# One trunk layer on one Trainium2 core: the first weight sums of the feed-forward computed during the output projection, low parts on VectorE, the first norm's vector spread by matmuls

## The chip, the core and the metric

The kernel runs on one core of a Trainium2 chip. Five engines work side by side, each with its own in-order instruction stream: TensorE (PE; its weight loads are listed apart as PEld), VectorE (DVE), ScalarE (ACT), GpSimd (POOL) and SyncE (SP), which here only issues DMA transfers. The metric is the device time of one execution in microseconds (us); lower is better.

## The reference, cut to what matters

```python
h = rmsnorm(x, norm_mix_pre)                      # x is 1024 x 1024, float32
proj = h @ w_in                                   # feeds convolution branch, attention, gates
...                                               # convolution branch, stick-breaking attention
merged = sigmoid(g_conv) * conv_out + sigmoid(g_att) * att_out
x = x + rmsnorm(merged @ w_out, norm_mix_post)    # output projection
h = rmsnorm(x, norm_ffn_pre)
gate, up = split(h @ w_ffn_up)                    # D_FF = 2816 = 22 blocks of 128
ff = (silu(gate) * up) @ w_ffn_down
x = x + rmsnorm(ff, norm_ffn_post)
```

## The kernel before

Every float32 product is made from three matmuls on rounded parts. An operand X is split into a high part (ScalarE copies X to the rounded type) and a low part (X minus the high part, a subtraction on VectorE or GpSimd); a step then adds high by high, high by low and low by high in PSUM. `mm3` writes these, twelve 128x512 matmuls for a product over four 128-row blocks.

The order of work is partly written out and partly made by a scheduler. Up to the feed-forward, the framework orders each engine's instructions from the program. From `up` on, the engines are wrapped in `Ordered`, so that the instructions keep the order in which the code issues them.

**First norm** (L148 to L190). `fetch(0)` loads the first 128 rows of x in two halves (`xts[0]`), the identity for transposes (`ident`) and the gain vector `gpre`, which one DMA copies to all 128 partitions; all are on SP's queue. `pre(tb)` squares block tb on ScalarE (L174, the sums go to `sst`), GpSimd takes the power to -0.5 (`pr`, L107), and VectorE multiplies by `pr` and `gpre` (L177). `transpose_split` transposes on PE and splits into `hH` and `hL`; `v_block` makes the first products `psv` (L139 to L141).

**Output projection** (L685 to L840). For each block tb of 128 tokens, `out_steps` makes `po`, and `post(tb)` adds the normed result to x (`x1`, L727 and L728) and writes the second normed block (`xr`, L736). `operands(tb - 2)` transposes an older block (`flip`). The feed-forward is a seven-product scheme on 2x2 blocks (Strassen's kind), so blocks 4 to 7 do not only give `hH`/`hL` but also the sums t1, t2 and t3: for each of these four blocks VectorE makes `s1`, `s2`, `s3` (L779 to L786), ScalarE rounds them (L788), and the low parts are taken at L789, t2's on VectorE, those of t1 (kept in `hL`) and t3 on GpSimd. `fetch_gate`, `prep_a` and `split` load and split the first gate weights `rg`; while `lows[0]` is GpSimd, all these low parts `wl` (L804, L835) are on GpSimd. PE meanwhile makes the first two of the seven products for f = 0, 1 and 2 (`early`).

**Feed-forward, up** (`up(f)`, 22 rounds). Round f has the products m5, m3, m6, m7, m4 besides its early m1 and m2 (for f > 0: m6, m5, m7, m3, m4). Their weights are sums of the gate and up blocks `rg` and `ru`: `sums_12` and `sums_34` (L894 to L900) followed by `split_12` and `split_34`. For f = 0 these stand under a high priority behind the output projection. `make_t4`, in round 0, makes the operand t4 from t2 and B21: twelve subtractions and additions `da`, `db` and four low parts on VectorE. Product m4 of round 0 needs it, and a free PSUM bank that VectorE's addition `u` gives back. From here on every engine's instruction has line L940.

**Last norm** (`evacuate`, last branch). For each of the last four blocks VectorE adds `c12` (tile `du`), ScalarE squares it (`junk`), VectorE multiplies it in place by the gain `gpo`, GpSimd takes the root, and VectorE scales and adds before the store.

Of the kernel before, what the change touches and what calls it, by code (L numbers as in the profile page):

```python
# [15 lines left out]
P = 128  # L16
# [21 lines left out]
def layer_kernel(ctx, tc, x, vecs, dww, gains, ident_d, mask_d, wv, wi, wbr, wo, wu, wdq, wd, out):  # L38
# [109 lines left out]
    vts = []  # L148
    with pool("prep") as pp:
        gpre = pp.tile([P, D], F32, name="gpre")  # L150
        wvt = []
        G.memset(mhalf, -0.5)
        xts = {}

        def parts_of(tb):
            return [slice(0, HALF), slice(HALF, D)] if tb == 0 else [slice(0, D)]

        def fetch(tb):
            xts[tb] = w4("xt")[:, 0:D]
            for cs in parts_of(tb):  # L160
                SP.dma_start(out=xts[tb][:, cs], in_=x[tb * P:(tb + 1) * P, cs])
            if tb == 0:
                SP.dma_start(out=ident, in_=ident_d)
                SP.dma_start(out=gpre, in_=gains[0:1, :].broadcast_to([P, D]))

        def pre(tb):
            if tb > 1:
                fetch(tb)
            xt = xts[tb]
            parts = parts_of(tb)  # L170
            junk = pp.tile([P, D], BF16, name="junk", tag="junk", bufs=1)
            sst = small("sst", 2)
            for n, cs in enumerate(parts):
                A.activation(out=junk[:, cs], in_=xt[:, cs], func=AF.Square, scale=ROOT, accum_out=sst[:, n:n + 1])  # L174
            r = power_of(sst[:, 0:1], 1, sst[:, 1:2] if tb == 0 else None)
            for cs in parts:
                V.scalar_tensor_tensor(out=xt[:, cs], in0=xt[:, cs], scalar=r, in1=gpre[:, cs], op0=ALU.mult, op1=ALU.mult)  # L177

        fetch(0)
        pre(0)  # L180
        fetch(1)
        transpose_split(psz, "z", xts[0], 0)
        wvt.append(load_w(wv[0, 0], pp, sub=V))
# [249 lines left out]
    def bank(nm):  # L433
        return ps8.tile([P, HALF], F32, name=nm, tag="d")
# [323 lines left out]
    def operands(tb):  # L758
        ps = slice((tb % 4) * P, (tb % 4) * P + P)

        def at_(t):
            return [o[:, :, ps] for o in t]

        def as_f32(t):
            return t.bitcast(F32)

        if tb < 4:
            for half, t in ((0, B11), (1, B21)):
                tp = flip(tb, half)
# [12 lines left out]
        tp = flip(tb, 1)
        A.activation(out=b22[0], in_=tp, func=AF.Copy)
        V.tensor_tensor(out=s2, in0=tp, in1=s1, op=ALU.subtract)
        V.tensor_tensor(out=b22[1], in0=tp, in1=as_f32(b22[0]), op=ALU.subtract)
        V.tensor_tensor(out=s3, in0=tp, in1=s3, op=ALU.subtract)  # L786
        for (h, l), src, eng in ((t2, s2, V), (t1, s1, G), (t3, s3, G)):
            A.activation(out=h, in_=src, func=AF.Copy)  # L788
            eng.tensor_tensor(out=l, in0=src, in1=as_f32(h), op=ALU.subtract)  # L789

# [2 lines left out]

    early = {}
    rgs, rus, ops = {}, {}, {}
    lows = [G]

    def split(src, pl, n=1024, low=None, tag="w", bufs=2):  # L800
        wh = pl.tile([P, n], F32R, name="wh", tag=f"{tag}h", bufs=bufs)
        wl = pl.tile([P, n], F32R, name="wl", tag=f"{tag}l", bufs=bufs)
        A.activation(out=wh, in_=src, func=AF.Copy)  # L803
        (low or lows[0]).tensor_tensor(out=wl, in0=src, in1=wh.bitcast(F32), op=ALU.subtract)  # L804
        return wh, wl

    def fetch_gate(f):
# [24 lines left out]
    raw2, wh2, wl2 = [op_.tile([P, 1024], dt, name=nm, tag="wh", bufs=6) for nm, dt in (("rg2", F32), ("wh2", F32R), ("wl2", F32R))]  # L832
    SP.dma_start(out=raw2, in_=wu[2])
    A.activation(out=wh2, in_=raw2, func=AF.Copy)
    G.tensor_tensor(out=wl2, in0=raw2, in1=wh2.bitcast(F32), op=ALU.subtract)  # L835
    ops[2] = {1: ((wh2, wl2), 0), 2: ((wh2, wl2), HALF)}
    operands(NT - 2)
    for f in range(3):
        early[f] = [bank("m1"), bank("m2")]
        prod(early[f][0], *ops[f][1], B11)  # L840
        if f == 2:
            pin[0] = True
            operands(NT - 1)
        prod(early[f][1], *ops[f][2], B21)
# [45 lines left out]
    def sums_12(f):  # L890
        rg, ru = rgs[f], rus[f]
        s12s[f] = fp.tile([P, 1024], F32, name="s12", tag="s", bufs=1)
        s1, s2 = s12s[f][:, 0:HALF], s12s[f][:, HALF:1024]
        V.tensor_tensor(out=s1, in0=ru[:, 0:HALF], in1=ru[:, HALF:1024], op=ALU.add)  # L894
        V.tensor_tensor(out=s2, in0=s1, in1=rg[:, 0:HALF], op=ALU.subtract)

    def sums_34(f):
        rg, ru, s2 = rgs[f], rus[f], s12s[f][:, HALF:1024]
        V.tensor_tensor(out=rg[:, 0:HALF], in0=rg[:, 0:HALF], in1=ru[:, 0:HALF], op=ALU.subtract)
        V.tensor_tensor(out=rg[:, HALF:1024], in0=rg[:, HALF:1024], in1=s2, op=ALU.subtract)  # L900

    def split_12(f):
        w = split(s12s[f], fp)
        ops[f][5], ops[f][6] = (w, 0), (w, HALF)

    def split_34(f):
        w = split(rgs[f], fp)
        ops[f][7], ops[f][3] = (w, 0), (w, HALF)

    def prep_c(f):  # L910
        ops[f][4] = (split(rus[f][:, HALF:1024], fp, HALF, tag="c", bufs=1), 0)

# [15 lines left out]
        for k, da in zip(ks, das):  # L928
            V.tensor_tensor(out=T4[1][:, k, :], in0=da, in1=T4[0][:, k, :].bitcast(F32), op=ALU.subtract)

    quads, s12s = {}, {}


    class Ordered:
# [222 lines left out]
    def root(sst):  # L1157
        return power_of(sst[:, 0:1], 1, sst[:, 1:2])
# [7 lines left out]
    def evacuate(i, p, ps):  # L1166
# [110 lines left out]
```

## Time and profile before

| | us |
|---|---|
| median of 3 runs | 1417.72 (1417.61 to 1420.14) |
| the profiled execution: its own time | 1417.84 |
| the profiled execution: span from first to last instruction | 1416.0 |
| PE busy in the span | 1363.2 (96%) |
| DVE busy | 1063.1 (75%) |
| ACT busy | 527.0 (37%) |
| POOL busy | 87.0 (6%) |

The profile is one execution. A busy share is a mean over stages. A row of the timeline gives an instruction's start, its duration, the engine, the line, what it writes and reads, and in brackets how long the engine had been idle and what ended that. "xt<-in_x" means that xt is written from in_x; buffer numbers are left out of names there.

### The profile page before, as it was taken

To read this page: it belongs to the slowest core of one execution; us is meant where nothing else is said; L and a number is where in the kernel's file an instruction comes from. 1 tells how busy PE (TensorE), PEld (TensorE's weight loads), DVE (VectorE), ACT (ScalarE), POOL (GpSimd) and SP (SyncE) were. 2 spreads that over 40 slices of the span, in tenths; PEclk is the share of its full clock that TensorE was granted. 3 is DMA by queue.
4 is the path that set the end of the run, shared out by engine and by line. 5 is a ranking of instruction groups with operands and counts; after the bars stand their busy time and mean duration, and the time that the engine had idled before them with its cause. 6 is when DMAs were issued, how large, how long until landed. Compare 5 with 4: busy or idle time off the path is not lost.

```text
span 1416.0 us, 17251 instructions
## 1 busy us (share of the span) xinstructions
PE 1363.2 (96%) x6412; PEld 1116.4 (79%) x6412; DVE 1063.1 (75%) x1560; ACT 527.0 (37%) x863; POOL 87.0 (6%) x208
## 2 busy tenths in 40 slices
PE   6999999999999999999998899999999999999997
PEld 6876787787877888888887678888888888788886
DVE  6599988886999967236549898888877876655565
ACT  6466656553102126123334323222222222533432
POOL 2100100000000000000117000000000000000102
PEclk9999999999999999999999999999999999999999
DMA  6011001100102121114322254444444434985373
GB/s 229 24 30 38 23 23 34 42 31 24 44 25 72 39 74 37 52 45 142 133 89 90 104 194 171 171 165 162 139 152 171 171 127 156 349 292 195 116 265 107
DMA packets 62403, 160.97 MB, mean 114 GB/s; under 512 B 6384, under 2 KB 17904, under 8 KB 62320
## 3 DMA queue, kind: packets, MB, share of 16 engines
q1 hardware_dynamic: 62032, 158.83, 32.9%
q8 instruction: 50, 0.82, 0.2%
q10 hardware_dynamic: 288, 1.05, 0.2%
q14 instruction: 33, 0.27, 0.1%
HBM read 117.65 MB, written 40.11 MB: 111 GB/s over the span
## 4 chain that ended last, share of the span: by engine, by line
PE 74%; DVE 16%; issue 3%; ACT 3%; DMA 2%; POOL 1%; SPq 0%; DVEq 0%; POOLq 0%; ACTq 0%
PE m L940 26%; PE md L940 13%; PE pg L82 4%; PE pg L80 4%; PE pg L79 4%; PE pb L82 2%; DVE R L262 2%; PE pb L80 2%; PE pb L79 2%; PE psg L82 2%; DVE R L257 2%; PE psg L80 2%; DVE p L469 2%; PE psg L79 2%; DVE aL L323 2%
## 5 line engine op out<-in xcount | busy, mean ns | idle before, releaser
L940 PE MATMUL m<-t,wh 128*128 128x512 f32 x528 | 133.8, 395 | 4.4 <-DVE u L940 2.9
L940 PE MATMUL m<-hH,wh 128*128 128x512 f32 x328 | 130.6, 398 | 4.4 <-ACT wh L803 4.4
L940 PE MATMUL m<-hL,wh 128*128 128x512 f32 x328 | 130.1, 397 | 0.0
L940 PEld LDWEIGHTS m<-t,wh 128*128 128x128 f32 x528 | 99.1, 188 | 29.2 <-issue 4.0
L940 PE MATMUL md<-wh 128*128 128x512 f32 x308 | 120.2, 390 | 1.1 <-ACT wh L940 1.1
L940 PE MATMUL md<-wl,wh 128*128 128x512 f32 x308 | 120.1, 390 | 0.9 <-DVE wl L940 0.9
L940 ACT ACTIVATE c<-c 128x512 f32<-128x512 f32 x44 | 27.8, 633 | 243.2 <-DVE c L940 243.2
L73 DVE TENSOR_TENSOR wl<-wraw,wh 128x1024 fp32r<-128x1024 f32 (+1 forms) x60 | 64.1, 1074 | 57.3 <-ACT wh L72 38.8
L72 ACT ACTIVATE wh<-wraw 128x1024 fp32r<-128x1024 f32 (+1 forms) x60 | 56.4, 945 | 123.7 <-PE pg L80 30.4
L79 PE MATMUL pg<-hH,wh 128*128 128x512 f32 x256 | 100.6, 393 | 0.0
L80 PE MATMUL pg<-hL,wh 128*128 128x512 f32 x256 | 99.7, 390 | 0.0
L940 PE MATMUL md<-wh,wl 128*128 128x512 f32 x308 | 97.4, 390 | 0.0
L940 DVE TENSOR_TENSOR wl<-ra,wh 128x1024 fp32r<-128x1024 f32 (+1 forms) x42 | 48.5, 1155 | 62.6 <-ACT wh L940 62.5
L940 PE MATMUL m<-hH,wl 128*128 128x512 f32 x328 | 89.8, 396 | 0.4 <-POOL wl L804 0.4
L469 DVE SCALAR_TENSOR_TENSOR p<-u,dw,p 128x513 f32<-128x513 f32 (+1 forms) x116 | 78.8, 737 | 0.0
L940 PEld LDWEIGHTS m<-hH,wh 128*128 128x128 f32 x328 | 62.2, 190 | 19.3 <-ACT wh L803 4.8
L940 PEld LDWEIGHTS m<-hH,wl 128*128 128x128 f32 x328 | 62.1, 189 | 15.2 <-POOL wl L804 0.8
L940 PEld LDWEIGHTS m<-hL,wh 128*128 128x128 f32 x328 | 62.2, 190 | 14.0
L940 ACT ACTIVATE wh<-ra 128x1024 fp32r<-128x1024 f32 (+1 forms) x42 | 41.4, 986 | 84.6 <-PE md L940 56.4
L940 PE MATMUL m<-t,wl 128*128 128x512 f32 x264 | 71.6, 394 | 0.0
L940 PEld LDWEIGHTS md<-wl,wh 128*128 128x128 f32 x308 | 57.8, 188 | 13.8 <-DVE wl L940 1.3
L940 PEld LDWEIGHTS md<-wh 128*128 128x128 f32 x308 | 57.8, 188 | 13.6 <-ACT wh L940 1.5
(233 smaller groups left out, 3231.7 us busy)
## 6 DMA issues: line engine op xcount, KB each, us to landing
ra<-act SPq DMA_DIRECT2D x35, 512.0 KB, 6.5
wraw<-in_wi SPq DMA_DIRECT2D x32, 512.0 KB, 3.6
rg<-in_wu SPq DMA_DIRECT2D x23, 512.0 KB, 4.8
ru<-in_wu SPq DMA_DIRECT2D x22, 512.0 KB, 5.6
q<-in_wdq SPq DMA_DIRECT2D x22, 512.0 KB, 6.4
wsum<-q SPq DMA_DIRECT2D x22, 512.0 KB, 2.6
act<-sa SPq DMA_DIRECT2D x44, 256.0 KB, 2.5
rb<-wsum SPq DMA_DIRECT2D x20, 512.0 KB, 9.7
```

What stands on the lines that cost most here:

```text
L72: A.activation(out=wh, in_=raw, func=AF.Copy)
L73: (sub or low_of[0]).tensor_tensor(out=wl, in0=raw, in1=wh.bitcast(F32), op=ALU.subtract)
L79: PE.matmul(ps, lhsT=lh, rhs=rh, start=(first and j == 0), stop=False)
L80: PE.matmul(ps, lhsT=lh, rhs=rl, start=False, stop=False)
L82: PE.matmul(ps, lhsT=ll, rhs=rh, start=False, stop=(last and j == n - 1))
L257: V.tensor_tensor_scan(out=R[:, 3:3 + n][:, ::-1], data0=d, data1=d, initial=1.0, op0=ALU.mult, op1=ALU.bypass)
L262: V.tensor_tensor_scan(out=R[:, 4:4 + n][:, ::-1], data0=d, data1=d, initial=carry, op0=ALU.mult, op1=ALU.bypass)
L323: V.tensor_tensor(out=flat[1][:, 0:n * P], in0=tpf, in1=flat[0][:, 0:n * P].bitcast(F32), op=ALU.subtract)
L469: V.scalar_tensor_tensor(out=to if last is None else last, in0=u[:, k:k + n], scalar=w, in1=to, op0=ALU.mult, op1=ALU.add)
L940: return lambda *a, **k: tc.keep_in_program_order(fn(*a, **k))
```

## The change

Four things change.

1. The gain vector of the first norm arrives as one row (`grow`, 4 KB on one partition). Two float32 matmuls of a row of ones with it spread it into two PSUM banks (`gps`); ScalarE copies these into `gpre`. Block 0 is multiplied by the PSUM banks themselves, the other blocks by `gpre`.
2. In `operands`, the low parts of t1 and t3 are taken by VectorE, in the order t1, t2, t3. `split` always uses VectorE for the low part, and so does the split of `rg2`. GpSimd is left with the powers to -0.5 and, in the last norm, with eight multiplications.
3. For f = 0 the up block is loaded into the output projection's pool (`ru0`), `sums_12(0)` and `sums_34(0)` are issued around `operands(6)`, and `split_12(0)` ahead of the early products of f = 1. `split_34(0)` stays where it was. The right half of the up block is loaded a second time behind it (`ru`), as `prep_c(0)` needs it unsummed.
4. In the last norm the multiplication by `gpo` writes another tile (`c22`) and no longer the tile that ScalarE squares.

```diff
-                SP.dma_start(out=gpre, in_=gains[0:1, :].broadcast_to([P, D]))
+                SP.dma_start(out=grow, in_=gains[0:1, :])
+                for n, cs in enumerate(parts_of(0)):
+                    PE.matmul(gps[n], lhsT=onerow, rhs=grow[:, cs], start=True, stop=True)
+                    A.activation(out=gpre[:, cs], in_=gps[n], func=AF.Copy)
...
-                V.scalar_tensor_tensor(out=xt[:, cs], in0=xt[:, cs], scalar=r, in1=gpre[:, cs], op0=ALU.mult, op1=ALU.mult)
+                V.scalar_tensor_tensor(out=xt[:, cs], in0=xt[:, cs], scalar=r, in1=gps[cs.start // HALF] if tb == 0 else gpre[:, cs], op0=ALU.mult, op1=ALU.mult)
...
-        for (h, l), src, eng in ((t2, s2, V), (t1, s1, G), (t3, s3, G)):
+        for (h, l), src in ((t1, s1), (t2, s2), (t3, s3)):
             A.activation(out=h, in_=src, func=AF.Copy)
-            eng.tensor_tensor(out=l, in0=src, in1=as_f32(h), op=ALU.subtract)
+            V.tensor_tensor(out=l, in0=src, in1=as_f32(h), op=ALU.subtract)
...
-        (low or lows[0]).tensor_tensor(out=wl, in0=src, in1=wh.bitcast(F32), op=ALU.subtract)
+        V.tensor_tensor(out=wl, in0=src, in1=wh.bitcast(F32), op=ALU.subtract)
...
-    G.tensor_tensor(out=wl2, in0=raw2, in1=wh2.bitcast(F32), op=ALU.subtract)
+    V.tensor_tensor(out=wl2, in0=raw2, in1=wh2.bitcast(F32), op=ALU.subtract)
     ops[2] = {1: ((wh2, wl2), 0), 2: ((wh2, wl2), HALF)}
+    rus[0] = op_.tile([P, 1024], F32, name="ru0", tag="wl", bufs=6)
+    SP.dma_start(out=rus[0], in_=wu[NFB])
+    sums_12(0, op_)
     operands(NT - 2)
+    sums_34(0)
     for f in range(3):
+        if f == 1:
+            split_12(0, wst)
...
-        fetch_up(0)
+        split_34(0)
+        rus[0] = fp.tile([P, 1024], F32, name="ru", tag="ru", bufs=2)
+        SP.dma_start(out=rus[0][:, HALF:1024], in_=wu[NFB, :, HALF:1024])
         fetch_up(1)
-        sums_12(0)
-        split_12(0)
-        sums_34(0)
-        split_34(0)
...
-            gained(1, c12[p], V)
-            finish(p, (c11[p], c12[p]), root(sst1[p]), xt)
+            V.tensor_tensor(out=c22[p], in0=c12[p], in1=gpo[:, HALF:D], op=ALU.mult)
+            finish(p, (c11[p], c22[p]), root(sst1[p]), xt)
```

VectorE's instructions at the start of the program, before. xt_103 and xt_118 are the first two blocks of x, `pv` the sum of squares that goes to GpSimd, `wl` the low part of a weight, `hL` that of a transposed half block:

```order
L105 TENSOR_SCALAR pv_112<-sst_109 128x1
L177 SCALAR_TENSOR_TENSOR xt_103<-xt_103,pr_114,gpre_101 128x512 x2
L103 TENSOR_SCALAR pv_143<-sst_141 128x1
L177 SCALAR_TENSOR_TENSOR xt_118<-xt_118,pr_145,gpre_101 128x1024
L73 TENSOR_TENSOR wl_137<-wraw_134,wh_136 128x1024
L118 TENSOR_TENSOR hL_79<-tp_120,hH_78 128x4x128
```

The same place after (the first two blocks are xt_108 and xt_127):

```order
L105 TENSOR_SCALAR pv_121<-sst_118 128x1
L103 TENSOR_SCALAR pv_152<-sst_150 128x1
L184 SCALAR_TENSOR_TENSOR xt_108<-xt_108,pr_123,gps_105 128x512
L73 TENSOR_TENSOR wl_146<-wraw_143,wh_145 128x1024
L184 SCALAR_TENSOR_TENSOR xt_108<-xt_108,pr_123,gps_106 128x512
L118 TENSOR_TENSOR hL_79<-tp_129,hH_78 128x4x128
L184 SCALAR_TENSOR_TENSOR xt_127<-xt_127,pr_154,gpre_101 128x1024
```

The multiplication of block 0 now stands behind the second block's sum of squares, and its second half behind the split of a weight. The whole first stage is woven anew in this way, on every engine; from the attention to the output projection the order of every engine is the same in both.

VectorE's instructions from the operands of the last block (`sums_6708`) to `make_t4`, before:

```order
L779 TENSOR_TENSOR sums_6708<-tp_6710,hH_78 128x512
L781 TENSOR_TENSOR sums_6708<-sums_6708,hL_79 128x512
L784 TENSOR_TENSOR sums_6708<-tp_6718,sums_6708 128x512
L785 TENSOR_TENSOR hL_79<-tp_6718,hH_78 128x4x128
L786 TENSOR_TENSOR sum3_6709<-tp_6718,sum3_6709 128x512
L789 TENSOR_TENSOR t2_5877<-sums_6708,t2_5877 128x4x128
L894 TENSOR_TENSOR s12_6812<-ru_6808 128x512
L895 TENSOR_TENSOR s12_6812<-s12_6812,rg_6152 128x512
L899 TENSOR_TENSOR rg_6152<-rg_6152,ru_6808 128x512
L900 TENSOR_TENSOR rg_6152<-rg_6152,s12_6812 128x512
L940 TENSOR_TENSOR c11_6833<-m2_6643,u2_6831 128x512
L940 TENSOR_TENSOR da_6868<-t2_5877,hH_78 128x512
```

The same place after, where the last block's sums are `sums_6728`; the four weight sums (L827 to L833) stand higher up, the last of them just ahead of the first row:

```order
L810 TENSOR_TENSOR wl_6685<-s12_6628,wh_6684 128x1024
L786 TENSOR_TENSOR sums_6728<-tp_6730,hH_78 128x512
...
L793 TENSOR_TENSOR sum3_6729<-tp_6738,sum3_6729 128x512
L796 TENSOR_TENSOR hL_79<-sums_6728,hH_78 128x4x128
L796 TENSOR_TENSOR t2_5886<-sums_6728,t2_5886 128x4x128
L796 TENSOR_TENSOR t3_5893<-sum3_6729,t3_5893 128x4x128
L810 TENSOR_TENSOR wl_6829<-rg_6161,wh_6828 128x1024
L810 TENSOR_TENSOR wl_6839<-ru_6832,wh_6838 128x512
L954 TENSOR_TENSOR c11_6844<-m2_6659,u2_6842 128x512
L954 TENSOR_TENSOR da_6879<-t2_5886,hH_78 128x512
```

The four sums have left the stretch between the last block's operands and `make_t4`; two more low parts of the operands and the low parts of two weights have come into it from GpSimd.

## Rows read from the trace of the kernel before

**Rows 1.** Windows: stretch, its us, then busy us (x instructions) of PE, PEld, DVE, ACT, POOL.

```profile
20.00:60.00 40.00, 39.54 (x278) 36.50 (x277) 21.98 (x36) 18.98 (x35) 9.42 (x25) 1.00 0.27 85
...
15.30:18.70 3.40, 3.40 (x17) 3.40 (x17) 3.33 (x5) 1.97 (x5) 0.55 (x1) 1.00 0.57 161
18.70:20.50 1.80, 1.80 (x16) 1.80 (x16) 0.32 (x2) 0.57 (x2) 0.00 (x0) 1.00 1.04 362
```

**Rows 2.** Timeline of the first 16 us: start, us, engine, line, operation.

```profile
2.12 0.43 SPq L164 DMA_DIRECT2D gpre<-in_gains  x1
...
8.25 1.42 DVE L177 SCALAR_TENSOR_TENSOR xt<-xt,pr,gpre 128x512 f32<-128x512 f32 x2 [3.23 <-DMA gpre<-in_gains]
...
9.06 1.97 PE L115 MATMUL tp<-ident,xt 128*128 128x128 f32 x8 [9.06 <-DVE xt L177]
9.51 1.06 ACT L174 ACTIVATE junk<-xt 128x1024 bf16<-128x1024 f32 x1 [4.73 <-DMA xt<-in_x]
```

**Rows 3.** DMA issues: what, queue, count, KB each, us from issue to landing.

```profile
gpre<-in_gains SPq DMA_DIRECT2D x1, 512.0 KB, 6.0
gpost<-in_gains SPq DMA_DIRECT2D x1, 512.0 KB, 3.7
...
ident<-in_ident SPq DMA_DIRECT2D x1, 64.0 KB, 2.6
```

**Rows 4.** Chain that ended last: two float32 matmuls, each two passes, start and us.

```profile
546.96 1.72 PE sp L590 x4
```

**Rows 5.** Timeline of PE at the feed-forward's start: the rows behind its idle times.

```profile
775.35 0.79 PE L940 MATMUL m<-hH,wh 128*128 128x512 f32 x1 [4.40 <-ACT wh L803]
...
792.21 2.48 PE L940 MATMUL m<-t,wh 128*128 128x512 f32 x8 [2.76 <-DVE u L940]
...
812.05 2.11 PE L940 MATMUL m<-t,wh 128*128 128x512 f32 x8 [1.10 <-ACT wh L940]
```

**Rows 6.** Windows of VectorE alone: stretch, its us, busy us (x instructions), granted clock.

```profile
743.00:768.00 25.00, 23.05 (x27) 1.00 0.30 109
768.00:792.10 24.10, 23.75 (x29) 0.86 0.25 87
...
771.80:778.60 6.80, 6.73 (x6) 0.60 0.26 77
```

**Rows 7.** Groups of VectorE (743 to 792.1 us) and GpSimd (739 to 784): count, busy us, mean ns.

```profile
L940 DVE TENSOR_TENSOR da<-da,db 128x512 f32<-128x512 f32 x4 | 4.8, 1211 | 0.1
L736 DVE SCALAR_TENSOR_TENSOR xr<-x,pr,gffn 128x1024 f32<-128x1024 f32 x2 | 4.6, 2307 | 0.9 <-POOL pr L107 0.9
L728 DVE TENSOR_TENSOR x<-x,xr 128x1024 f32<-128x1024 f32 x2 | 4.3, 2175 | 0.0
L781 DVE TENSOR_TENSOR sums<-sums,hL 128x512 f32<-128x512 f32 x3 | 3.7, 1234 | 0.1
L789 DVE TENSOR_TENSOR t<-sums,t 128x512 fp32r<-128x512 f32 x4 | 3.5, 886 | 0.0
...
L107 POOL TENSOR_TENSOR pr<-pv,mhalf 128x1 f32<-128x1 f32 x4 | 3.7, 931 | 9.6 <-DVE pv L105 6.5 <-DVE pv L103 3.1
```

**Rows 8.** Timeline of the same stretch: two VectorE rows beside GpSimd, one without.

```profile
743.27 5.78 POOL L804 TENSOR_TENSOR wl<-rg,wh 128x1024 fp32r<-128x1024 f32 x2
...
743.63 3.13 DVE L728 TENSOR_TENSOR x<-x,xr 128x1024 f32<-128x1024 f32 x1
746.69 0.68 DVE L785 TENSOR_TENSOR hL<-tp,hH 128x512 fp32r<-128x512 f32 x1
...
757.52 1.22 DVE L728 TENSOR_TENSOR x<-x,xr 128x1024 f32<-128x1024 f32 x1
```

**Rows 9.** Timeline of the last block's end on VectorE.

```profile
1408.57 0.69 DVE L940 TENSOR_TENSOR du<-md,du 128x512 f32<-128x512 f32 x1 [1.14 <-PE md L940]
...
1410.10 0.69 DVE L940 TENSOR_TENSOR du<-du,gpo 128x512 f32<-128x512 f32 x1 [0.85 <-ACT junk L940]
1410.71 0.21 DVE L940 TENSOR_SCALAR pv<-ss 128x1 f32<-128x1 f32 x1
```

More of the change, by code (lines that the diff above doesn't have):

```diff
@@ L150, in layer_kernel @@
         gpre = pp.tile([P, D], F32, name="gpre")
+        grow = pp.tile([1, D], F32, name="grow")
+        onerow = pp.tile([1, P], F32, name="onerow")
+        G.memset(onerow, 1.0)
+        gps = [pst.tile([P, HALF], F32, name="gps", tag="tp") for _ in range(2)]
         wvt = []
@@ L797, in layer_kernel, with split @@
     rgs, rus, ops = {}, {}, {}
-    lows = [G]
-    def split(src, pl, n=1024, low=None, tag="w", bufs=2):
+    def split(src, pl, n=1024, tag="w", bufs=2):
         wh = pl.tile([P, n], F32R, name="wh", tag=f"{tag}h", bufs=bufs)
@@ L813, in prep_a, with sums_12, sums_34, split_12 @@
         ops[f] = {1: (w, 0), 2: (w, HALF)}
+    s12s = {}
+    def sums_12(f, pl=None):
+        rg, ru = rgs[f], rus[f]
+        s12s[f] = pl.tile([P, 1024], F32, name="s12", tag="wl", bufs=6) if pl else fp.tile([P, 1024], F32, name="s12", tag="s", bufs=1)
+        s1, s2 = s12s[f][:, 0:HALF], s12s[f][:, HALF:1024]
+        V.tensor_tensor(out=s1, in0=ru[:, 0:HALF], in1=ru[:, HALF:1024], op=ALU.add)
+        V.tensor_tensor(out=s2, in0=s1, in1=rg[:, 0:HALF], op=ALU.subtract)
+    def sums_34(f):
+        rg, ru, s2 = rgs[f], rus[f], s12s[f][:, HALF:1024]
+        V.tensor_tensor(out=rg[:, 0:HALF], in0=rg[:, 0:HALF], in1=ru[:, 0:HALF], op=ALU.subtract)
+        V.tensor_tensor(out=rg[:, HALF:1024], in0=rg[:, HALF:1024], in1=s2, op=ALU.subtract)
+    def split_12(f, pl=None):
+        w = split(s12s[f], pl or fp)
+        ops[f][5], ops[f][6] = (w, 0), (w, HALF)
+    def split_34(f):
+        w = split(rgs[f], fp)
+        ops[f][7], ops[f][3] = (w, 0), (w, HALF)
     for tb in range(2):
@@ L888, in fetch_up @@
         SP.dma_start(out=rus[f], in_=wu[f + NFB])
[L890 to L908, printed above, removed]
     def prep_c(f):
@@ L929, in make_t4 @@
             V.tensor_tensor(out=T4[1][:, k, :], in0=da, in1=T4[0][:, k, :].bitcast(F32), op=ALU.subtract)
-    quads, s12s = {}, {}
+    quads = {}
     class Ordered:
@@ L1108, in layer_kernel @@
     PE, V, A, G, SP = [Ordered(e) for e in (PE, V, A, G, SP)]
-    lows[0] = V
     for f in range(NFB):
```

## Prediction

> **What bounds the kernel now.** I read the windows by stage first: from 20 to 60 us PE is busy for 39.54 of 40 us [rows 1], and so it is in most later stages, so a gain counts only where PE waits, and a shift made there is carried to the end. The engine orders show the change at three places alone: the first 50 us, the 50 us around 768, and the last norm. I then read the timeline at each.
>
> At the start, VectorE's first multiplication sat idle for 3.23 us until the gain vector landed, at 8.25 [rows 2]; its transfer took 6.0 us from issue at 2.12, thus to 8.1 [rows 2, 3]. ScalarE's square of the second block waited for x until 9.51 [rows 2]. PE is gapless only from 15.3 [rows 1].
>
> At the feed-forward's start PE waits 4.40, 2.76 and 1.10 us, on weights' high parts from ScalarE and on VectorE's `u` [rows 5]. VectorE was busy for 23.05 of 25 and 23.75 of 24.1 us there [rows 6]: it is the bound from 743 to about 818, and ScalarE's `wh` are late only because VectorE's sums were. But the load is swollen. The addition of x takes 3.13 us while GpSimd subtracts, 1.22 while it is quiet [rows 8].
>
> At the end, VectorE waits 0.85 us for the square before it multiplies in place [rows 9].
>
> **The feed-forward's start.** What goes from VectorE: the swelling. Against the row of 1.22 for a wide addition [rows 8], the two L728 lose (2.18 - 1.22) x 2 = 1.9 us; the two L736, against the 1.42 that two halves of the same form take [rows 2], (2.31 - 1.42) x 2 = 1.8; three L781 and four L789 and four `da`, against 0.68 for a narrow one [rows 8], (1.23 - 0.68) x 3 = 1.7, (0.89 - 0.68) x 4 = 0.8 and (1.21 - 0.68) x 4 = 2.1 [rows 7]; the four weight sums, 6.73 us together [rows 6], against 4 x 0.68 = 2.7, lose 4.0. Sum 12.3.
>
> What comes: eight narrow low parts (t1, t3 of four blocks) and that of `ru`, nine at 0.68 [rows 8] less the 0.07 by which neighbours overlap in the dense rows of the timeline, 9 x 0.61 = 5.5; five wide ones (f = 0, 1, 2, and both splits), 1.22 less the same, 5 x 1.14 = 5.7. Sum 11.2. The instruction stream of before is idle for 49.1 - 46.8 = 2.3 us [rows 6], half of it waits for the power on GpSimd, which then queued behind its own subtractions; about 1 us of that goes, as other rows now stand in the gaps.
>
> Net by this account: 12.3 - 11.2 + 1.0 = 2.1 us earlier at `u`. Walking the new order row by row with steps of 0.60 (narrow) and 1.14 (wide) from 743.0, 45.6 us in place of 49.0, gives 3.4. I take the middle, 2.8, and 0 and 5 as bounds, since both accounts move rows of one execution into gaps that it doesn't show.
>
> Where it lands: in the new order the four sums and the split of m5's weights stand ahead of the last block's operands. So by the walk the first of these starts at 770.5, t1's low part, which m5 needs, ends near 774.4, and m5's wait shrinks by 1 us only (775.35 before). The product behind that wait may again be slow, as it was. That costs nothing: m4 is the next wait, and it hangs on `make_t4` and `u`, at 788.7 to 790.0 for 792.1. PE has the four products before it done by 788 even if m5 takes 5 us. The cover is 1 us; without it, that much of the gain goes. Behind m4, PE waited 1.10 us at 812.05 on the same VectorE chain [rows 5], which moves up as a whole; no more is won there. The second load of `ru` stands on SP's queue until the sum L832 has read its space, about 765.5; ahead of the next `ru` and `q`. A 512 KB transfer took 3.7 us [rows 3], so it lands by 769, wanted at 775. Its cost is nothing; if it came 5 us late, VectorE's chain would slip by the excess. GpSimd's powers run without a queue and cost less.
>
> GpSimd keeps four powers in the stretch, 0.93 us each before [rows 7]. A subtraction with one operand in PSUM kept its 0.68 us beside GpSimd's work [rows 8], so not every VectorE row can be held up by them, and the multiplication that follows a power waits for its result anyway: nothing taken off here, 3.7 us at most.
>
> The Trainium skill (SBUF — State Buffer, section Who interferes with whom) says that a VectorE instruction with two SBUF inputs contends with a GpSimd instruction that reads SBUF, and that whichever is second waits for the whole of the first. By it the powers that stay would still hold VectorE up, and the middle could come out as low as 2.8 - 3.7 = -0.9; that is rival (e) below.
>
> **The last norm.** The multiplication no longer waits for the square, but runs beside it. The sum `pv`, which needs the square, comes at 1410.10 for 1410.71 [rows 9]: 0.6 us, all on the path, since nothing but root, scaling and store follows. Bounds 0.4 to 0.8.
>
> **The start.** The 512 KB spread goes; 4 KB come, two matmuls and two copies. Two float32 matmuls took 1.72 us [rows 4]; at the slower rate of the first 18 us, double. The row lands like the 64 KB of `ident`, 2.6 us [rows 3], at 4.7, so the halves are ready by 6.5 and 8.2. Now the cost: VectorE's first multiplication stands behind the second block's sum of squares, thus behind the landing T of x's second block. Without the spread, T is between 5.6 (`ident` at 4.25 and 1.3 us for 512 KB, the distance of the landings at 8.1 and 9.4) and 8.1 (9.4 less that 1.3). For the low end speaks that the spread was alone between 4.25 and 8.1, three times 1.3; against it, that a like spread, `gpost`, took an ordinary 3.7 us later [rows 3]. I take 6.5. From T the path is the square 1.25, a copy 0.6, the weight's high part 1.06 and low part 1.2, half a multiplication 0.7: PE runs without a gap from T + 4.8 = 11.3, for 15.3 before, but has then 12 transposes still to do that were done before, 12 x 0.25 = 3.0 [rows 2]. That is 15.3 - 14.3 = 1.0 us. Besides, 17 instructions took 3.40 us up to 18.7 and 16 took 1.80 behind it [rows 1]: TensorE ran at half rate, its 1.2 GHz level, until 3.4 us after it had become gapless (the granted-clock column shows 1.00 there; the durations tell it). If it rises as long after the new gapless start, about 3 us of slow work take 1.7: 1.3 more. 2.3 together; 3.2 with T = 5.6, 0.7 with T = 8.1, and less wherever VectorE, whose split now stands between, leaves PE waiting. I take 2.0, bounds -0.7 (T = 8.1, no gain by rate) to 3.2. PE is full up to 60 us, so it is carried on.
>
> **Sum.** 2.8 + 2.0 + 0.6 = 5.4. The profiled execution took 1417.84, 1.8 more than its span; 1417.84 - 5.4 = 1412.4, and the median is 0.1 lower: 1412.3, which is 0.38% less.
>
> **Rivals.** (a) The spread took only its bytes' share: T = 8.1, start 0.7: 1413.6. For it speaks the row of `gpost` [rows 3]; against it the 3.9 us between two landings. (b) VectorE's added work is not paid back in time: the four sums and three wide low parts ahead of the last block make m5 and `make_t4` no earlier, middle 0: 1415.1. For it, VectorE's share of 95% and m5's small gain; against, both accounts. (c) Slower: the swelling is not GpSimd's doing but comes with two-operand reads in a busy stretch, and stays. Then VectorE has 11.2 us more before `u` and PE's wait for m4 grows by as much: 1417.7 + 11.2 - 2.6 = 1426.3 (it has the start's and the last norm's gain). It decides from about 2.6 us of net slip on. Against it the same addition at 1.22 us in the same stretch with GpSimd quiet [rows 8]. (d) The start loses: T near 9.4 as before, everything hangs behind it, -2 us: 1416.3. (e) The four powers on GpSimd go on holding VectorE up for all their 3.7 us [rows 7]: middle -0.9, 1416.0.
>
> **How the numbers follow.** Forecast 54% (1410 to 1413.5), a 18%, b 11%, d 6%, e 4%, c 4%, better than 1410 (start 3.2, middle 4 or more) 3%. Leaving out c and d, 10%, and taking in half of the best cases, the range is 1409.5 to 1416.0. About 0.2%, 2.8 us, is what can be told from no change: faster than 1414.9 has the forecast, the best, a and a third of b: 0.78; within, the rest of b, d and e and a little more: 0.17; slower: 0.05.
>
> **What would show it.** In the profile after: T as the ScalarE square's start, near 6.5, and PE gapless from 11 to 12; the wide additions at 1.22 in the stretch of 743 to 770; m4 and `u` 2.1 to 3.4 us earlier, beyond the start's shift; GpSimd with few rows there; `pv` right behind the square's sum at the end. I am wrong if VectorE's rows stay long without GpSimd, if the square still starts past 8, or if PE waits longer for m4 than 2.8 us.

## The result, and the profile of the changed kernel

The changed kernel takes 1411.81 us (median of four runs, 1411.01 to 1412.78) where the kernel before took 1417.88 (1417.61 to 1420.14) beside it: a ratio of 0.9949, 95% interval 0.9937 to 0.9960. Forecast were 1412.3. The profiled execution took 1412.78 with a span of 1411.0, for 1417.84 and 1416.0.

The start, in the timeline (start, us, engine, line, operation, and in brackets the idle time before and what ended it), which answers to [rows 2]:

```profile
4.14 3.75 PE L170 MATMUL gps<-grow,onerow 1*128 1x512 f32 x4 [4.14 <-DMA grow<-in_gains]
...
6.83 1.06 ACT L181 ACTIVATE junk<-xt 128x1024 bf16<-128x1024 f32 x1 [2.17 <-DMA xt<-in_x]
...
8.56 0.75 DVE L184 SCALAR_TENSOR_TENSOR xt<-xt,pr,gps 128x512 f32<-128x512 f32 x1 [0.39 <-ACT gpre L171]
...
9.36 1.12 PE L115 MATMUL tp<-ident,xt 128*128 128x128 f32 x4 [1.47 <-DVE xt L184]
...
11.16 0.58 PE L139 MATMUL psv<-wh,hH 128*128 128x256 f32 x1 [0.69 <-ACT hH L117]
```

ScalarE's square of x's second block starts at 6.83 for 9.51, and the last idle time of TensorE's start ends at 11.16. Further on, the first `kst` row on VectorE (L219 before, L226 after) comes at 49.48 for 52.17, and the first `sums` row of the feed-forward's preparation at 737.02 for 739.85: the start gave 2.7 us, 2.8 when the middle begins. The two `kst` rows, before and after:

```profile
52.17 0.68 DVE L219 TENSOR_TENSOR kst<-psk,kst 64x512 fp32r<-64x512 f32 x1 [5.28 <-ACT kst L218]
49.48 0.69 DVE L226 TENSOR_TENSOR kst<-psk,kst 64x512 fp32r<-64x512 f32 x1 [5.29 <-ACT kst L225]
```

TensorE's waits at the feed-forward's start, same view, which answers to [rows 5]:

```profile
770.01 0.50 PE L954 MATMUL m<-hH,wh 128*128 128x512 f32 x1 [2.32 <-ACT hH L795]
771.93 0.50 PE L954 MATMUL m<-hL,wh 128*128 128x512 f32 x1 [1.43 <-DVE hL L796]
786.31 2.06 PE L954 MATMUL m<-t,wh 128*128 128x512 f32 x8 [1.66 <-DVE u L954]
790.58 2.08 PE L954 MATMUL m<-t,wh 128*128 128x512 f32 x8 [1.31 <-DVE u L954]
806.08 2.11 PE L954 MATMUL m<-t,wh 128*128 128x512 f32 x8 [1.17 <-ACT wh L954]
812.44 2.12 PE L954 MATMUL m<-t,wh 128*128 128x512 f32 x8 [0.34 <-ACT wh L954]
```

m4 starts at 786.31 for 792.21, which is 5.90 earlier; less the 2.83 from the start, the middle gave 3.07. The waits themselves did not go: m5's 4.40 is now 2.32 + 1.43, m4's 2.76 is 1.66, and a new one of 1.31 stands behind it. What moved is the VectorE chain that ends them. Its groups (count, busy us, mean ns) from 740 to 786 us, and GpSimd's from 737, which answer to [rows 7, 8]:

```profile
L954 DVE TENSOR_TENSOR da<-da,db 128x512 f32<-128x512 f32 x4 | 2.8, 692 | 0.1
L743 DVE SCALAR_TENSOR_TENSOR xr<-x,pr,gffn 128x1024 f32<-128x1024 f32 x2 | 2.6, 1286 | 0.6 <-POOL pr L107 0.4
L735 DVE TENSOR_TENSOR x<-x,xr 128x1024 f32<-128x1024 f32 x2 | 2.4, 1220 | 0.0
L788 DVE TENSOR_TENSOR sums<-sums,hL 128x512 f32<-128x512 f32 x3 | 2.1, 685 | 0.0
...
L107 POOL TENSOR_TENSOR pr<-pv,mhalf 128x1 f32<-128x1 f32 x4 | 2.8, 708 | 22.2 <-DVE pv L103 11.8 <-DVE pv L105 10.4
```

No row is swollen any more: 692 ns for 1211, 1286 for 2307, 1220 for 2175, 685 for 1234. The end, which answers to [rows 9]:

```profile
1404.28 0.69 DVE L954 TENSOR_TENSOR du<-md,du 128x512 f32<-128x512 f32 x1 [2.06 <-PE md L954]
1405.01 0.69 DVE L954 TENSOR_TENSOR dc<-du,gpo 128x512 f32<-128x512 f32 x1
1405.07 0.63 ACT L954 ACTIVATE junk<-du 128x512 bf16<-128x512 f32 x1 [6.85 <-DVE du L954]
...
1405.82 0.21 DVE L954 TENSOR_SCALAR pv<-ss 128x1 f32<-128x1 f32 x1
```

From the sum's add to `pv` it is 1.54 us for 2.14: 0.60. The three gains make 6.5, but the spans differ by 5.0. The rest is lost in the down projection, behind a pair of TensorE waits that both kernels have, here before and after:

```profile
1213.09 0.50 PE L940 MATMUL md<-wh 128*128 128x512 f32 x1 [1.10 <-ACT wh L940]
1214.54 0.50 PE L940 MATMUL md<-wl,wh 128*128 128x512 f32 x1 [0.95 <-DVE wl L940]
...
1207.13 0.49 PE L954 MATMUL md<-wh 128*128 128x512 f32 x1 [1.09 <-ACT wh L954]
1208.58 0.50 PE L954 MATMUL md<-wl,wh 128*128 128x512 f32 x1 [0.96 <-DVE wl L954]
```

Windows (stretch, its us, busy us of PE, PEld, DVE, ACT, POOL, then the granted clock) of the 5 us behind that pair, first of the kernel before:

```profile
1214.50:1219.50 5.00, 4.96 (x22) 4.12 (x23) 3.65 (x4) 2.19 (x4) 0.00 (x0) 1.00 1.01 359
```

and of the changed kernel:

```profile
1208.50:1213.50 5.00, 4.92 (x14) 3.91 (x15) 3.68 (x5) 2.24 (x4) 0.00 (x0) 0.66 1.00 357
```

The mean granted clock of 0.66 says that TensorE was at its lower level, 1.2 GHz, for part of that stretch; it did 14 products for 22. From the second of the two waits to the last `du` row it is 195.70 us (1208.58 to 1404.28) for 194.03 (1214.54 to 1408.57): 1.67 lost. 2.83 + 3.07 + 0.60 - 1.67 = 4.83, and 0.07 more came between `u` and the last wait at 812.44.

### The profile page after: what moved, and what is told of

The parts are those of the page before. It is cut to its first block, busy times and chain, and to the rows that moved or that the text cites. A ratio compares the mean times of both kernels' runs of the same rounds, so it can differ in the third digit from the quotient of the medians.

```text
span 1411.0 us, 17263 instructions
## 1 busy us (share of the span) xinstructions
PE 1364.9 (97%) x6416; PEld 1116.3 (79%) x6416; DVE 1062.3 (75%) x1574; ACT 527.2 (37%) x865; POOL 58.3 (4%) x195
## 3 DMA queue, kind: packets, MB, share of 16 engines
q10 hardware_dynamic: 288, 1.05, 0.2%
## 4 chain that ended last, share of the span: by engine, by line
PE 72%; DVE 19%; issue 3%; ACT 2%; DMA 1%; POOL 0%; SPq 0%; DVEq 0%; POOLq 0%; ACTq 0%
PE m L954 27%; PE md L954 13%; DVE p L476 4%; PE pg L82 3%; PE pg L80 3%; PE pg L79 3%; DVE R L269 2%; PE pb L82 2%; PE pb L80 2%; DVE R L264 2%; PE pb L79 2%; PE psg L82 2%; DVE aL L330 2%; PE po L702 1%; PE po L704 1%
## 5 line engine op out<-in xcount | busy, mean ns | idle before, releaser
L954 DVE TENSOR_TENSOR wl<-ra,wh 128x1024 fp32r<-128x1024 f32 (+1 forms) x42 | 48.5, 1154 | 64.2 <-ACT wh L954 63.9
```

The source lines that it names most:

```text
L954: return lambda *a, **k: tc.keep_in_program_order(fn(*a, **k))
```

## The experiments

Readings taken from every profile, in us: the start of ScalarE's square of x's second block (T); the first `kst` row behind it; from the first `sums` row to `u`, the addition that m4 waits for; the first of the two waits in the down projection; from the second of them to the last `du`.

| kernel | T | `kst` | `kst` - T | `sums` to `u` | wait | to `du` |
|---|---|---|---|---|---|---|
| before | 9.51 | 52.17 | 42.66 | 51.53 | 1.10 | 194.03 |
| middle alone | 10.10 | 53.12 | 43.02 | 48.43 | 0.85 | 194.11 |
| low parts alone | 10.60 | 53.16 | 42.56 | 48.65 | 1.61 | 195.84 |
| early sums alone | 10.65 | 52.24 | 41.59 | 51.79 | 0.73 | 194.04 |
| changed | 6.83 | 49.48 | 42.65 | 48.46 | 1.09 | 195.70 |
| changed, again | 7.70 | 50.03 | 42.33 | 48.43 | 1.21 | 195.67 |
| start and last norm | 8.01 | 51.12 | 43.11 | 51.52 | 1.05 | 194.03 |
| GpSimd subtracts beside | 7.42 | 50.03 | 42.61 | 50.89 | 0.83 | 194.02 |
| GpSimd copies beside | 7.50 | 50.19 | 42.69 | 49.47 | 1.14 | 195.72 |
| spread beside | 10.39 | 52.64 | 42.25 | 48.45 | 0.90 | 194.02 |

**Start and last norm alone, middle alone.** The change was cut in two along its places: the edits of lines 148 to 184 and of the last `evacuate` branch in one kernel, all the rest in the other.

> The kernel before with the start's edit and the last norm's alone; the feed-forward's start stays as it was. My theory: the three places are independent, so the start gives the 2.7 us that the first rows of `kst` and `ql` show (52.17 to 49.48, 57.56 to 54.86), the last norm 0.6 (time from the last `du<-md,du` to `pv` 2.14 to 1.54 us), and the three waits of TensorE at the feed-forward's start stay near 4.4, 2.8 and 1.1: 1417.8 - 3.3 = 1414.5. Rival: the middle is set by something that does not move with the start, so its waits grow by what the start won and only the last norm's 0.6 is left: 1417.2. A third term that I had not forecast, a stretch at the lower clock after the pair of waits in the down projection, can add 1.7 in any run.

> The kernel before with the edits of the feed-forward's start alone (low parts on VectorE, early sums); start and last norm as they were. My theory: `u` and the wait for m4 come 3.1 us earlier than before (788.3 for 791.4), m5 waits about 3.7 in two pieces, the wide additions of x take 1.22 us: 1417.8 - 3.1 = 1414.7. Rival: part of the 3.1 us came from the start's shift (another phase of the scheduler or of the transfers), so here it is under 1.5: 1416.3 or more.

Measured: 1414.92 (ratio 0.9976, 0.9966 to 0.9986) and 1415.13 (0.9979, 0.9970 to 0.9988), against 1418.0 for the kernel before. TensorE's idle times of the first, then of the second:

```profile
773.43 0.79 PE L947 MATMUL m<-hH,wh 128*128 128x512 f32 x1 [4.39 <-ACT wh L810]
...
790.30 2.06 PE L947 MATMUL m<-t,wh 128*128 128x512 f32 x8 [2.76 <-DVE u L947]
```

```profile
773.74 0.58 PE L947 MATMUL m<-hH,wh 128*128 128x512 f32 x1 [2.31 <-ACT hH L788]
775.67 0.79 PE L947 MATMUL m<-hL,wh 128*128 128x512 f32 x1 [1.35 <-DVE hL L789]
790.03 2.08 PE L947 MATMUL m<-t,wh 128*128 128x512 f32 x8 [0.84 <-DVE u L947]
```

With the start alone the old waits stand to the hundredth (4.39, 2.76) and everything comes earlier by what the start won, in this profile (T of 8.01) 1.05 us at `kst` and 1.90 from `sums` on; with the middle alone the stretch from `sums` to `u` is 48.43, as in the full change. The gains are 3.1 and 2.9 us, and 6.1 for both together: the parts add up, and the rival, in which the middle eats the start's gain, is out.

**Low parts alone, early sums alone.** In the first, the kernel before has only this changed:

```diff
-        for (h, l), src, eng in ((t2, s2, V), (t1, s1, G), (t3, s3, G)):
+        for (h, l), src in ((t1, s1), (t2, s2), (t3, s3)):
...
-            eng.tensor_tensor(out=l, in0=src, in1=as_f32(h), op=ALU.subtract)
+            V.tensor_tensor(out=l, in0=src, in1=as_f32(h), op=ALU.subtract)
...
-    lows = [G]
+    lows = [V]
...
-    G.tensor_tensor(out=wl2, in0=raw2, in1=wh2.bitcast(F32), op=ALU.subtract)
+    V.tensor_tensor(out=wl2, in0=raw2, in1=wh2.bitcast(F32), op=ALU.subtract)
```

The second has the middle of the change with these lines undone.

> The kernel before with only the low parts moved from GpSimd to VectorE; the first weight sums stay where they were, behind the last block. My theory: the swelling of VectorE's rows is GpSimd's subtractions, so it goes here as well: the wide additions of x take 1.22 us, the four weight sums 0.68 each, and VectorE has the same work up to `u` as in the full change. Then `u` is as early as there, 2 to 3 us before 791.4, and 1417.8 - 2.5 = 1415.3, with a wait for m5 of 4 to 6 us that the products behind it hide. Rival: the early sums carry the gain, since they take m5's weights off the end: then 0 to -1 here, 1417 to 1419.

> The full change of the feed-forward's start with the low parts put back on GpSimd: early sums alone. Start and last norm as before. My theory: the swelling stays (additions of x near 2.2 us, the sums over 1.2 us each where GpSimd subtracts), VectorE is full, and `u` does not come earlier by more than 0.5 us: 1417.3. The rival, that the early sums carry the gain: `u` 2 to 3 us earlier, 1415.3.

Measured: 1415.63 (0.9985, 0.9976 to 0.9994) and 1418.21 (0.9999, 0.9990 to 1.0008). The groups of VectorE from 740 to 792 us, low parts alone:

```profile
L940 DVE TENSOR_TENSOR da<-da,db 128x512 f32<-128x512 f32 x4 | 2.8, 690 | 0.1
L736 DVE SCALAR_TENSOR_TENSOR xr<-x,pr,gffn 128x1024 f32<-128x1024 f32 x2 | 2.6, 1285 | 0.6 <-POOL pr L107 0.4
L728 DVE TENSOR_TENSOR x<-x,xr 128x1024 f32<-128x1024 f32 x2 | 2.4, 1220 | 0.0
```

and early sums alone:

```profile
L781 DVE TENSOR_TENSOR sums<-sums,hL 128x512 f32<-128x512 f32 x4 | 4.9, 1216 | 0.1
L736 DVE SCALAR_TENSOR_TENSOR xr<-x,pr,gffn 128x1024 f32<-128x1024 f32 x2 | 4.6, 2305 | 0.9 <-POOL pr L107 0.9
L728 DVE TENSOR_TENSOR x<-x,xr 128x1024 f32<-128x1024 f32 x2 | 4.4, 2179 | 0.0
```

Moving nine narrow and five wide subtractions to an engine that was 95% busy made its chain 2.88 us shorter (48.65 for 51.53); moving the sums ahead alone made it 0.26 longer, and with the low parts moved it is worth 0.2. The gain of the middle is the low parts', and it comes from where they left.

**GpSimd given work again.** To the changed kernel, behind the low parts of T1 and T3 of the four later blocks; the tile is read by nobody, and no other engine's order changes:

```diff
+    beside = op_.tile([P, 4, P], F32, name="beside")
...
+            if src is not s2:
+                G.tensor_tensor(out=beside, in0=as_f32(h), in1=as_f32(h), op=ALU.subtract)
```

and in a second kernel `G.tensor_copy(out=beside, in_=as_f32(h))` in its place.

> The changed kernel, with GpSimd given work beside it again: in each of the four later blocks two subtractions of 128x512 from SBUF into a tile that nobody reads, eight in all, with the order of every other engine as in the changed kernel. It separates the cause of the swelling. My theory, that GpSimd's subtraction holds up VectorE's two-operand rows: the eight take 1.3 us each, and VectorE's SBUF-with-SBUF rows beside them go from 0.68 to 1.2 or more; with some 60 per cent of 10.4 us falling on such rows, `u` slips by 3 to 6 us (from 48.5 us behind the first `sums` row to 52 to 54) and the time is 1411.8 + 3 to 6 = 1415 to 1418. The rival of my prediction, that the long rows come with a busy stretch of two-operand reads: 0.68 stays 0.68, `u` stays, 1411.8. A second rival, that GpSimd is the one that waits (its rows grow, VectorE's don't): 1411.8 as well, with GpSimd's rows over 2 us.

> The same with eight copies of 128x512 by GpSimd (one SBUF operand read, one written) in place of the subtractions. If any read of SBUF by GpSimd holds VectorE up, the rows of 0.68 grow as with the subtractions and `u` slips by 3 to 6 us: 1415 to 1418. If it takes two operands on GpSimd's side, VectorE's rows stay at 0.68: 1411.8.

Measured: 1415.0 (0.9971, 0.9960 to 0.9982) with the subtractions, 1413.53 (0.9965, 0.9952 to 0.9979) with the copies; the cleaner reading is the stretch from `sums` to `u`, 2.4 and 1.0 us longer. Both are less than the 3 to 6 us that I expected, and the copies are neither of the two cases that I had set down. In the profile with the subtractions, GpSimd's rows and then VectorE's:

```profile
767.24 3.63 POOL L799 TENSOR_TENSOR beside<-t 128x512 f32<-128x512 f32 x1 [0.96 <-ACT t L796]
772.22 1.04 POOL L799 TENSOR_TENSOR beside<-hH 128x512 f32<-128x512 f32 x1 [1.35 <-ACT hH L796]
774.21 1.29 POOL L799 TENSOR_TENSOR beside<-t 128x512 f32<-128x512 f32 x1 [0.95 <-ACT t L796]
```

```profile
768.75 1.22 DVE L813 TENSOR_TENSOR wl<-s,wh 128x1024 fp32r<-128x1024 f32 x1
769.88 0.69 DVE L787 TENSOR_TENSOR sums<-tp,hH 128x512 f32<-128x512 f32 x1
...
773.92 0.69 DVE L797 TENSOR_TENSOR t<-sums,t 128x512 fp32r<-128x512 f32 x1
774.52 1.53 DVE L797 TENSOR_TENSOR t<-sum,t 128x512 fp32r<-128x512 f32 x1
```

Either engine waits for the other. The subtraction at 772.22 runs beside rows with an operand in PSUM and takes 1.04. The one at 774.21 came just ahead of `t<-sum,t`, which reads two tiles of SBUF: that row took 1.53 in place of 0.68 and ended 0.55 us behind GpSimd's end (775.50). The one at 767.24 came while VectorE went from one such row to the next, and took 3.63: it ended at 770.87, 1.0 us after VectorE reached a row with a PSUM operand (769.88), so it had waited through four VectorE rows and not for one. With the copies the same VectorE row grows, by less:

```profile
772.72 0.88 POOL L799 COPY beside<-t 128x512 f32<-128x512 f32 x1 [1.38 <-ACT t L796]
773.04 1.10 DVE L797 TENSOR_TENSOR t<-sum,t 128x512 fp32r<-128x512 f32 x1
```

All the growth can be counted: four VectorE rows with the subtractions (2.06 for 1.29, twice 1.53 for 0.68, 0.81 for 0.69), 2.6 us together, and three with the copies (1.61 for 1.29, twice 1.10 for 0.68), 1.2 us. The Trainium skill (SBUF — State Buffer, section Who interferes with whom) states this exclusion for a VectorE instruction with two SBUF inputs beside a GpSimd instruction that reads SBUF; the trace agrees, and shows it for a plain copy too. That whichever is second waits for the whole of the first, as the prediction has it, is too little for the row at 767.24: it waited for four. So the rival in which the long rows belong to the busy stretch is out: the same rows in the same order are long with GpSimd and short without. My expected slip was too large, since I had counted VectorE as the one that waits in 60% of GpSimd's time; in part it was GpSimd, and in part the rows beside it had an operand in PSUM.

**The spread as a transfer alone.** To the changed kernel, read by nobody:

```diff
                 SP.dma_start(out=grow, in_=gains[0:1, :])
+                spread = pp.tile([P, D], F32, name="spread")
+                SP.dma_start(out=spread, in_=gains[0:1, :].broadcast_to([P, D]))
```

> The changed kernel with the 512 KB spread of the gain vector issued again at its old place, into a tile that nobody reads; the multiplication still takes the matmuls' halves. It separates the transfer from the wait on its result. My theory: the spread itself delays all that is queued behind it, so the square of x's second block starts at 9.5 to 10.7 again, as in the four profiles with the old start, for 6.8 and 8.0 in the two with the new one, and the first rows of `kst` come at 52 to 53 us: the start's gain is gone, 1411.8 + 2.4 = 1414.2. Rival: what was won is the wait for the vector; the square starts before 8.5, `kst` before 51.2, 1411.8.

Measured: 1413.54 (0.9965, 0.9951 to 0.9979). The time alone doesn't decide, as this interval overlaps that of the changed kernel (0.9937 to 0.9960); the timeline does:

```profile
7.06 0.75 DVE L186 SCALAR_TENSOR_TENSOR xt<-xt,pr,gps 128x512 f32<-128x512 f32 x1 [2.01 <-ACT gpre L173]
...
10.39 1.06 ACT L183 ACTIVATE junk<-xt 128x1024 bf16<-128x1024 f32 x1 [3.43 <-DMA xt<-in_x]
```

VectorE had its gain vector in time, at 7.06, and it did not help: T is 10.39, as with the old start, and `kst` 52.64. So the wait for the vector, the 3.23 us of [rows 2], was never what the start hung on; the place of the 512 KB ahead of x's second block was. The table says the same without an experiment: `kst` follows T by 41.6 to 43.1 us in all ten profiles. The mean T is 10.2 in the four with the old start and 7.5 in the five with the new one, `kst` 52.7 and 50.2.

**The changed kernel again, and a version that goes on.** From the readings two costs were left: VectorE's first multiplication stood behind the second block and behind ScalarE's copy of the same bank (the 0.39 us above), and `make_t4` recombined T2 from its parts. In the core (`t2s` is the float32 sum of T2, kept until then; T2's low parts are now taken in `make_t4`; besides, `grow` is fetched ahead of x and the copies stand behind the second block):

```diff
-            for cs in parts:
-                V.scalar_tensor_tensor(out=xt[:, cs], in0=xt[:, cs], scalar=r, in1=gps[cs.start // HALF] if tb == 0 else gpre[:, cs], op0=ALU.mult, op1=ALU.mult)
+            for cs in (parts if tb > 1 else parts_of(0)):
+                V.scalar_tensor_tensor(out=xt[:, cs], in0=xt[:, cs], scalar=r, in1=gps[cs.start // HALF] if tb < 2 else gpre[:, cs], op0=ALU.mult, op1=ALU.mult)
...
-            V.tensor_tensor(out=da, in0=T2[0][:, k, :].bitcast(F32), in1=B21[0][:, k, :].bitcast(F32), op=ALU.subtract)
-            V.tensor_tensor(out=db, in0=T2[1][:, k, :].bitcast(F32), in1=B21[1][:, k, :].bitcast(F32), op=ALU.subtract)
-            V.tensor_tensor(out=da, in0=da, in1=db, op=ALU.add)
...
+            V.tensor_tensor(out=da, in0=t2s[:, k, :], in1=B21[0][:, k, :].bitcast(F32), op=ALU.subtract)
+            V.tensor_tensor(out=da, in0=da, in1=B21[1][:, k, :].bitcast(F32), op=ALU.subtract)
```

> The changed kernel and two steps on. At the start the vector's row is fetched first, x's first two blocks take the halves from PSUM, and the copies for later blocks come behind them, so that VectorE's first multiplication hangs neither on the second block's landing nor on ScalarE's copy. In the middle the float32 sum for T2 is kept, so that T4 takes two VectorE subtractions a piece in place of three operations: four rows of 0.68 less, and T2's low parts move out of the way of m5. By my account VectorE is the bound up to `u`, so `u` comes 4 x 0.62 = 2.5 us earlier behind the first `sums` row (46.0 for 48.5), and the two waits there (1.66 and 1.31) take up 2.5 of their 3.0 us. Start: all eight transposes done before the first product and that at about 9.7 to 10.5 us, `kst` 1 to 2 us earlier than 49.5 to 51.1. Together 3.5 to 4.5: 1407.3 to 1408.3. Rival: TensorE or the banks are the bound behind m5 and the start hangs on T alone: 0 to 1, 1411.

> The changed kernel unaltered, beside the two that follow, for a comparison on one chip. My theory of its start: everything hangs on the landing of x's second block, so the first `kst` row comes 42.2 to 43.1 us behind the start of ScalarE's square of that block, wherever this falls between 6.8 and 8.0. The middle takes 48.4 to 48.5 us from the first `sums` row to `u`, as in the two profiles that have it. Time 1411.8 to 1413. Whether the stretch at the lower clock follows the pair of waits in the down projection is open: two of six profiles had it, at 1.7 us.

> The first version with four VectorE rows less and the other start, again, on the same chip as the changed kernel. By the profiles it should be 1.9 us ahead in the middle (46.6 for 48.5 us from the first `sums` row to `u`) and 0.7 at the start at an equal landing: 2.6 us below the changed kernel's median of this call. Rival: what was won in the middle is lost behind it, since TensorE then waits 3.2 us at the next bank: level with the changed kernel.

Measured: 1410.6 (0.9944, 0.9930 to 0.9957) at first; then, on one chip, 1411.26 (0.9948, 0.9936 to 0.9961) for the changed kernel and 1411.23 (0.9938, 0.9925 to 0.9952) for this version. The forecast of 1407.3 to 1408.3 was missed. In its two profiles `u` comes 46.59 and 46.57 us behind `sums`, for 48.4 to 48.5: 1.9 us won, where 2.5 were expected. `kst` is 41.9 behind T, some 0.7 less than before, but at 49.45 and 50.20 no 1 to 2 us earlier, since T was 7.51 and 8.34. On one chip the medians are 0.03 us apart, so the times don't tell it from the changed kernel; whether the profiles' gain is there in the mean of the runs is not shown. VectorE's idle times behind `u` in the first profile:

```profile
787.51 1.23 DVE L961 TENSOR_TENSOR wl<-s,wh 128x1024 fp32r<-128x1024 f32 x1 [1.13 <-ACT wh L961]
...
792.08 0.69 DVE L961 TENSOR_TENSOR a<-c,c 128x512 f32<-128x512 f32 x1 [0.70 <-ACT c L961]
...
795.19 1.23 DVE L961 TENSOR_TENSOR wl<-rg,wh 128x1024 fp32r<-128x1024 f32 x1 [1.21 <-ACT wh L961]
```

Each time VectorE waits for ScalarE on work it has only just handed over. The last version puts other rows of its own there:

```diff
                 sums_12(nf)
+                t4_low(t4_rest)
                 split_12(nf)
...
+        if f == 0:
+            sums_34(nf)
         a2 = half_tile("a2", "a", 4)
         V.tensor_tensor(out=a2, in0=up2, in1=gate2, op=ALU.mult)
-        if f == 0:
-            sums_34(nf)
         if more:
-            split_34(nf)
+            split_34(nf, (lambda: weight_sums(0)) if f == 0 else None)
...
-        if f == 0:
-            weight_sums(f)
```

> The same with VectorE's rows behind it put in another order, nothing added or taken away: `u` and the first sums of the next weights ahead of T4's low parts, the next sums ahead of the multiplication that waits for the gate, the sums of the down weights in the wait for the high part. In the last version VectorE was idle there for 1.13, 0.70 and 1.21 us, waiting for ScalarE. My theory: VectorE is the bound up to the last wait (811.34), so these 3.0 us go, TensorE's waits of 3.17, 1.27, 1.18 and 0.33 us shrink by as much, and the time is 2 to 3 us below the last version. Rival: TensorE's own products and the eight banks set the pace behind 785: 0 to 1 us.

Measured: 1406.87 (0.9914, 0.9900 to 0.9927), whose interval lies below that of the changed kernel on the same chip and just overlaps that of the version before. 2 to 3 us below that version were expected, the medians are 4.4 apart. TensorE's idle times behind m5:

```profile
781.66 0.47 PE L966 MATMUL m<-t,wh 128*128 128x512 f32 x1 [0.75 <-ACT t L966]
783.50 2.31 PE L966 MATMUL m<-t,wh 128*128 128x512 f32 x7 [1.36 <-DVE t L966]
787.13 0.47 PE L966 MATMUL m<-t2h,wh 128*128 128x512 f32 x1 [0.38 <-DVE u L966]
```

The waits of 1.18 and 0.33 us behind 800 are gone, and those up to there are 2.49 together: 3.5 us less than the four of the first profile (3.17, 1.27, 1.18, 0.33). Against the profile of the version before on the same chip, the span is 7.0 us shorter: 0.9 at the start, 4.6 from `sums` to the first wait in the down projection (464.1 for 468.7; 1.3 of it is that wait, 0.30 for 1.63, and 3.3 the reordering), and 1.5 since the stretch at the lower clock stayed away. So the 3.0 us of idle time came out in full. What makes up the rest of the 4.4 us between the medians is open: start and clock vary from run to run of one kernel, and whether the shorter wait belongs to the new order is not shown (it was 1.54 and 1.63 in both profiles of the version before).

## Why the prediction was right, step by step

- **What bounds the kernel.** VectorE up to `u`, TensorE elsewhere: confirmed by the two half changes, whose shifts are carried on to the last `du` to within 0.3 us (1.90 to 1.93 from `sums`, 2.18 to 2.41 from `u`).
- **The feed-forward's start, forecast 2.8, bounds 0 to 5.** Measured 3.07 in the profile, 3.10 with the middle alone. The walk (3.4) was nearer than the account (2.1). The swelling went as a whole. The point at which the last block's operands start, 770.5 by the walk, is 770.7 when the start's 2.83 is put back to 767.88. m5's wait shrank by 0.65, forecast 1. "Behind m4 no more is won" held only as a sum: m4's wait fell by 1.10, and the next one rose from 0.17 to 1.31. The second load of `ru` left SP's queue at 762.70, and nothing waited for it.
- **The start, forecast 2.0, bounds -0.7 to 3.2.** Measured 2.7 to 2.8 in the pair of profiles, 2.5 between the means. That all hangs on T was right. The last gap ended at 11.16 for 11.3 forecast, but by two errors: T was 6.83 for 6.5, and the path behind it 4.33 for 4.8. T was taken too early for every run: five profiles have 6.83 to 8.01. The old start's T of 9.51, to which I compared it, is the earliest of four (to 10.65). Both T were taken too early, which nearly cancels in their difference; which T a single profile shows is chance. The steps on transposes and rate were not needed, since `kst` follows T by nearly the same before and after (means 42.5 and 42.7 us).
- **The last norm, forecast 0.6.** Measured 0.60 in every profile that has it.
- **Rival (c)**, swelling without GpSimd: out, by the work given back to GpSimd. **(b)**: out, the added rows were paid back (48.65 for 51.53 with them alone). **(d)**: out, and **(a)** too, though one T (8.01, with a gain of 1.05 at `kst` over the profile of before) came close to it. That T is also just past the 8 that I named as a sign of being wrong; `sums` was 1.90 earlier even so. **(e)**: out, though the rule it rests on holds. No VectorE row grew beside a power; in this kernel the power is the second. Two of the four took 0.55 us beside rows with a PSUM operand, the others 0.87 and 0.86 beside a row with two tiles of SBUF.
- **What was not in the sum:** the 1.67 us at the lower clock. The three terms came to 6.5 in place of 5.4, and this loss brought the profile back to 5.0. The medians differ by 6.1. Both profiles of the changed kernel have the loss, the one of the kernel before has not. That the forecast lies 0.5 us from the measured median is partly luck: two of the terms were too small, and a loss was missing.

## What to carry to other kernels

Where a busy VectorE has rows of one form at several durations, look at what GpSimd does beside the long ones before taking work off VectorE: giving VectorE more work can shorten its chain. At a start, look for what all else follows at a fixed distance, and price a transfer by what is queued behind it; the wait that names it may be covered. When the bound engine's idle times each wait for work it has just given away, put ready rows of its own there first.

## What the runs showed of the hardware

- The granted clock fell behind the pair of waits in the down projection in some profiles and not in others. The first wait was 0.30, 0.73, 0.83, 0.85, 0.90, 1.05 and 1.10 us where it stayed at 1.00, and 1.09, 1.14, 1.21, 1.61 and 1.63 where it fell to 0.66 to 0.69 (mean over the next 5 us), which cost 1.5 to 1.8 us. Behind one of 1.54 it stayed at 1.00. 1.09 and 1.10 are on different sides, so the wait's length alone does not decide it, and what does is open. Behind m5's waits it fell too (0.60 in [rows 6], 0.79 from 772 to 780 us in the changed kernel) and cost nothing, as m4 then waited for `u` in any case.
- A GpSimd instruction can be held up by several VectorE rows with two SBUF operands that follow each other: 3.63 us for 1.04 with the subtractions, 3.22 for 0.61 with the copies, until a row with an operand in PSUM came.
- At the start TensorE did 19 products in 4.04 us without a gap and 42 in the next 4.80, while the granted-clock column (the third from the right) has 1.00 for both. Products of one form (`psv`, 128x256) started every 0.21 us up to 14.53 and every 0.12 us from 16.39 on. So the durations show the lower rate at the start and this column does not. Windows of the changed kernel:

```profile
11.16:15.20 4.04, 4.04 (x19) 4.04 (x20) 3.76 (x6) 2.42 (x4) 0.20 (x1) 1.00 0.63 191
15.20:20.00 4.80, 4.79 (x42) 4.58 (x41) 3.85 (x6) 4.18 (x8) 1.49 (x2) 1.00 0.71 271
```
